# Moving modulation-weight chunks from TensorE to VectorE in a two-layer diffusion trunk step (60 to 116 of 192)

## The chip, the cores and the metric

The kernel runs on one core of a Trainium2 chip. The metric is device time in microseconds for one execution of the whole program; lower is better.

## The reference: what is computed

Two layers over 128 context and 128 latent tokens, width 2048, all in fp32. Each layer has six modulation vectors of 2048 features for each of two conditioning vectors, then attention and a squared-ReLU MLP, each between modulated norms:

```python
def modulation(cvec, w_ada_l, b_ada_l):
    m = jax.nn.silu(cvec) @ w_ada_l + b_ada_l
    return jnp.split(m[:, None, :], N_MOD, axis=-1)
...
sh_a, sc_a, gt_a, sh_m, sc_m, gt_m = modulation(c, w_ada[l], b_ada[l])
h = rms_norm(xs, g_pre_a) * (1.0 + sc_a) + sh_a
...
xs = xs + gt_a * rms_norm(o, g_post_a)
h = rms_norm(xs, g_pre_m) * (1.0 + sc_m) + sh_m
xs = xs + gt_m * rms_norm(squared_relu_mlp(h, w_up[l], w_down[l]), g_post_m)
```

`w_ada` of one layer is 2048 x 12288, so the modulation is a product of two rows with 201 MB of weights over both layers: 192 chunks of 128 x 2048 fp32 (1 MB). The attention mixes three head groups (neighbourhood, grouped-query, differential) and one output projection.

## The kernel before

**Chunks.** Everything that is streamed comes in 1 MB chunks: 360 "trunk" chunks (projection in, projection out, MLP up and down) and 192 modulation chunks. SyncE's queue (SP) loads them in one fixed order into five buffers `raw` (`issue`, L994 to L1001); a load is issued when the chunk in its buffer is released. For a trunk chunk, `split_to` (L1003) makes of each half a high part `wh` on ScalarE (L1011) and the residue `wl` on VectorE (L1012), three buffers each, and TensorE multiplies three times (L361 to L363 with tokens stationary, L395 to L397 with weights stationary).

**Modulation on TensorE** (`ada_mm`, L126): 132 chunks. Four fp32 matmuls of 128 x 32 by 128 x 512 fill the four column strips of the array (L131). In the trace each of them is two rows, so a chunk is x8 there; in the order of a program it is x4. After four chunks ScalarE copies the bank to `pt` (L135), and TensorE transposes it (scale and shift) or, for a gate block, sums it with a selector (L153). 12 of the 132 chunks are held in idle `XT` buffers (`ahead`, L749).

**Modulation on VectorE** (`dv_mul`, L196): 60 chunks, in the two MLPs only. The weights lie transposed, features on partitions; `sB` holds silu(c) of both vectors on every partition. One chunk is four products of 1024 columns with a running sum (L204): two vectors by two halves. The last one writes back into `raw` and releases it.

**Order.** A list `items` fixes the order of the program, and each engine works through its own instructions in that order, apart from shifts that the scheduler of the framework makes when it builds the program. `weave` (L765) spreads modulation chunks evenly among the trunk chunks of a stretch. Attention, and `dv_mul`, are generators that are advanced by some steps after each half trunk chunk (L1054 to L1056):

```python
step_list(fast, 1)
step_list(slow, 2)
step_list(dvq, 1 + (len(dvq) > 1))
```

`slow` is attention and `dvq` the VectorE chunks. Before `w_out` may read a head group, `need` (L857) runs that group's generator to its end.

**Stages.** Layer 0 builds its normalized input a quarter at a time (`make_xt`), with the modulation blocks just ahead of it; all four input groups therefore finish late, and its attention runs from about 244 us to 413 us, beside the last input groups and the first part of `w_out`. Layer 1 has its modulation ready and runs group after group. x is stored to DRAM at the start of each MLP (`store_x`) and read back near its end (`load_x`), since `sB` takes two of the four `stg` buffers there.

Of the kernel before, what the change touches and what calls it, by code (L numbers as in the profile page):

```python
# [12 lines left out]
BF16 = mybir.dt.bfloat16  # L13
# [6 lines left out]
L = 2  # L20
# [17 lines left out]
C_ID, C_SEL, C_GC, C_GS, C_DC, C_DS, C_MK, C_LO, C_SV, C_END = 0, 128, 160, 288, 416, 480, 544, 608, 609, 865  # L38


def _consts():
    c = np.zeros((P, C_END), np.float32)
    c[:, C_ID:C_ID + P] = np.eye(P, dtype=np.float32)
    for g in range(4):
        for v in range(2):
            c[32 * g + v, C_SEL + v] = c[32 * g + v, C_SEL + 2 + v] = 1.0
# [22 lines left out]
def trunk(ctx: ExitStack, tc: tile.TileContext, I, O):  # L69
# [31 lines left out]
    def rstd(out, ss, n, width):  # L101
        """out = (ss / n + eps) ** -0.5"""
# [20 lines left out]
    # ---------------------------------------------------------------- ada  # L123
# [14 lines left out]
    gcs = {}  # L138

    def ada_post(l, sec, blk, pt):  # L140
        if sec in (2, 5):
            w = 0 if sec == 2 else 1
            if blk == 0:
                gb = sb([P, 512], "gb")
                gg = sb([P, 512], "gg")
                nc.sync.dma_start(gb, I["gb"][l, w])
                nc.sync.dma_start(gg, I["gg"][l, w])
                gcs[(l, w)] = (sb([P, 512], "gc", dt=F32R), gb, gg)
            gc, gb, gg = gcs[(l, w)]
            yield  # L150
            m = psm()
            r = slice(32 * blk, 32 * blk + 32)
            pe.matmul(m[r, :], cs[:, C_SEL:C_SEL + 32], pt, start=True, stop=True, tile_position=(0, 32 * blk))  # L153
            yield
            t, h = sb([P, 512], "tmp", NTMP), sb([P, 512], "tmp", NTMP, F32R)
            dve.tensor_tensor(t[r, :], m[r, :], gb[r, :], ALU.add)
            dve.tensor_tensor(t[r, :], t[r, :], gg[r, :], ALU.mult)
            act.activation(h[r, :], t[r, :], AF.Copy)
            dve.scalar_tensor_tensor(gc[r, :], h[r, :].bitcast(F32), cs[r, C_LO:C_LO + 1], t[r, :], ALU.mult, ALU.add)
        else:  # L160
            yield
            m = psm()
            for j in range(4):
                tr(m[:, j * P:(j + 1) * P], pt[:, j * P:(j + 1) * P])
            yield
            red = st1[:, 0:8].rearrange("p (j v) -> p j v", v=2)
            dve.tensor_reduce(red, m.rearrange("p (j g c) -> p j c g", g=4, c=32)[:, :, 0:2, :], AX.X, ALU.add)
# [17 lines left out]
    # the same product on the vector engine: features on partitions, c along the free axis  # L185
    sB = [None, None]
    dv_live = {}

    def load_sb():
        for v in range(2):  # L190
            sB[v] = sb([P, D], "stg", 4)
# [941 lines left out]
```

## Time and profile before

| what | us |
|---|---|
| median of 3 runs | 2409.05 (2407.94 to 2409.51) |
| profiled execution, its span | 2406.6 |
| TensorE busy (matmuls) | 2337.6 |
| VectorE busy | 1489.0 |
| ScalarE busy | 1109.7 |

The span runs from the first to the last instruction of one profiled execution. It is 2.45 us below the median; the three runs carry no trace, and a row of the trace is always one of the profiled execution. Busy time is the time in which an engine had at least one instruction under way. In rows of matmuls in time, the second number is a modelled duration; what a matmul adds to its neighbours is read from the distance of starts. In the MLPs DMA moved 203 to 279 GB/s, in layer 0's attention stage about 300.

### The profile page before, as it was taken

How to read it: one execution, taken by the hardware profiler on the slowest of the kernel's cores; microseconds unless marked ns; L12 is line 12 of the kernel's file. 1: busy time of each engine (PE TensorE's matmuls, PEld its weight loads, DVE VectorE, ACT ScalarE, POOL GpSimd, SP SyncE). 2: the span in 40 equal slices, each digit the busy share in tenths (PEclk: the TensorE clock that was granted, in tenths of full speed). 3: DMA queues.
4: the chain of work that ended last, by engine and by line, in shares of the span. 5: the costliest groups of instructions: out<-in, count | busy, mean ns of one | idle time of the engine just before them, and what ended most of it. 6: DMA issues, size and time to landing. Idle time of an engine off the chain costs nothing.

```text
span 2406.6 us, 33407 instructions
## 1 busy us (share of the span) xinstructions
PE 2337.6 (97%) x13584; PEld 1898.3 (79%) x13584; DVE 1489.0 (62%) x2078; ACT 1109.7 (46%) x1533; POOL 22.8 (1%) x30
## 2 busy tenths in 40 slices
PE   6999999989999999999999999999999999999998
PEld 3666666679789789889867777777988988988986
DVE  2455765367867878878455565546665566565545
ACT  3433454365444444435445454547544543543543
POOL 0000000000000000000000000000000000000000
PEclk8999999999999999999999999999999999999999
DMA  9778788876877877777676765776566566556652
GB/s 362 277 308 303 286 313 306 324 269 244 316 265 291 291 276 282 283 293 275 225 283 217 248 219 210 288 262 245 208 214 226 195 219 226 200 211 228 235 184 88
DMA packets 93650, 613.45 MB, mean 255 GB/s; under 512 B 13880, under 2 KB 16312, under 8 KB 20280
## 3 DMA queue, kind: packets, MB, share of 16 engines
q1 hardware_dynamic: 92776, 610.70, 69.5%
q8 instruction: 106, 1.74, 0.3%
q10 hardware_dynamic: 720, 0.62, 0.1%
q14 instruction: 48, 0.39, 0.0%
HBM read 599.49 MB, written 11.79 MB: 254 GB/s over the span
## 4 chain that ended last, share of the span: by engine, by line
PE 93%; DVE 2%; ACT 2%; DMA 1%; issue 1%; POOL 0%; ACTq 0%; POOLq 0%; DVEq 0%
PE acc L361 18%; PE acc L362 18%; PE acc L363 18%; PE acc L395 10%; PE acc L397 10%; PE acc L396 10%; PE ada L131 4%; PE m L107 2%; DVE wl L1012 1%; PE m L483 1%; DMA ngT<-ngT_in 1%; PE m L153 0%; PE m L517 0%; ACT stg L331 0%; PE m L302 0%
## 5 line engine op out<-in xcount | busy, mean ns | idle before, releaser
L1012 DVE TENSOR_TENSOR wl<-raw,wh 128x1024 fp32r<-128x1024 f32 x720 | 876.2, 1223 | 590.8 <-ACT wh L1011 586.9
L1011 ACT ACTIVATE wh<-raw 128x1024 fp32r<-128x1024 f32 x720 | 760.3, 1059 | 978.1 <-PE acc L363 615.2
L395 PE MATMUL acc<-XT,wh 128*128 128x256 f32 x2048 | 580.8, 284 | 2.8 <-ACT XT L277 2.8
L397 PE MATMUL acc<-XT,wl 128*128 128x256 f32 x2048 | 579.0, 283 | 0.5 <-DVE wl L1012 0.5
L396 PE MATMUL acc<-XT,wh 128*128 128x256 f32 x2048 | 577.8, 282 | 0.3 <-DVE XT L278 0.3
L361 PE MATMUL acc<-wh,big 128*128 128x512 f32 x1280 | 508.4, 400 | 0.0
L362 PE MATMUL acc<-wl,big 128*128 128x512 f32 x1280 | 506.0, 395 | 0.5 <-DVE wl L1012 0.5
L363 PE MATMUL acc<-wh,big 128*128 128x512 f32 x1280 | 505.0, 395 | 0.0
L395 PEld LDWEIGHTS acc<-XT,wh 128*128 128x128 f32 x2048 | 387.0, 189 | 14.0 <-issue 8.6
L396 PEld LDWEIGHTS acc<-XT,wh 128*128 128x128 f32 x2048 | 387.5, 189 | 0.7 <-DVE XT L278 0.5
L397 PEld LDWEIGHTS acc<-XT,wl 128*128 128x128 f32 x2048 | 386.7, 189 | 0.7 <-DVE wl L1012 0.7
L361 PEld LDWEIGHTS acc<-wh,big 128*128 128x128 f32 x1280 | 240.4, 188 | 80.9 <-issue 24.8
L363 PEld LDWEIGHTS acc<-wh,big 128*128 128x128 f32 x1280 | 240.9, 188 | 56.6 <-issue 0.7
L362 PEld LDWEIGHTS acc<-wl,big 128*128 128x128 f32 x1280 | 241.1, 188 | 55.8 <-DVE wl L1012 2.5
L361 PE MATMUL acc<-wh,XT 128*128 128x512 f32 x576 | 236.9, 414 | 9.5 <-ACT XT L277 7.0
L362 PE MATMUL acc<-wl,XT 128*128 128x512 f32 x576 | 230.0, 399 | 0.8 <-DVE wl L1012 0.7
L363 PE MATMUL acc<-wh,XT 128*128 128x512 f32 x576 | 228.3, 398 | 0.0
L361 PEld LDWEIGHTS acc<-wh,XT 128*128 128x128 f32 x576 | 109.0, 190 | 72.6 <-issue 25.6
L131 PE MATMUL ada<-raw,sT 128*32 128x512 f32 x960 | 136.6, 618 | 13.6 <-ACT sT L120 7.8
L204 DVE SCALAR_TENSOR_TENSOR tmp<-raw,stg 128x1024 bf16<-128x1024 f32 x120 | 144.8, 1218 | 2.5 <-DMA raw<-w_adaT_in 2.3
L204 DVE SCALAR_TENSOR_TENSOR raw<-raw,stg 128x1024 f32<-128x1024 f32 x120 | 145.4, 1219 | 0.1
L362 PEld LDWEIGHTS acc<-wl,XT 128*128 128x128 f32 x576 | 109.7, 190 | 27.3 <-DVE wl L1012 3.5
(140 smaller groups left out, 1243.7 us busy)
## 6 DMA issues: line engine op xcount, KB each, us to landing
raw<-w_up_in SPq DMA_DIRECT2D x128, 1024.0 KB, 4.8
raw<-w_down_in SPq DMA_DIRECT2D x128, 1024.0 KB, 4.8
raw<-w_ada_in SPq DMA_DIRECT2D x120, 1024.0 KB, 6.5
raw<-w_in_in SPq DMA_DIRECT2D x72, 1024.0 KB, 4.8
raw<-w_adaT_in SPq DMA_DIRECT2D x60, 1024.0 KB, 4.9
raw<-w_out_in SPq DMA_DIRECT2D x32, 1024.0 KB, 4.8
XT<-w_ada_in SPq DMA_DIRECT2D x12, 1024.0 KB, 8.8
xd<-stg SPq DMA_DIRECT2D x6, 1024.0 KB, 9.0
```

Of the source, the lines that this page charges most:

```text
L107: pe.transpose(out, in_, ident)
L131: pe.matmul(pa[32 * g:32 * g + 32, :], sT[:, 4 * kq + g, :], raw[:, g * 512:(g + 1) * 512], start=(kq == 0), stop=(kq == 3), tile_position ...
L204: dve.scalar_tensor_tensor(o, raw[:, c], 1.0, sB[v][:, c], ALU.mult, ALU.mult, accum_out=a[:, j, v, h:h + 1])
L361: pe.matmul(a, xh, wh[:, c], start=first, stop=False)
L362: pe.matmul(a, xh, wl[:, c], start=False, stop=False)
L363: pe.matmul(a, xl, wh[:, c], start=False, stop=last)
L395: pe.matmul(a, wh[:, c], xh, start=first, stop=False)
L396: pe.matmul(a, wh[:, c], xl, start=False, stop=False)
L397: pe.matmul(a, wl[:, c], xh, start=False, stop=last)
L483: pe.matmul(m[:, i * keys:(i + 1) * keys], qT[:, h, :], kT(h), start=True, stop=True)
L1011: act.activation(wh, r, AF.Copy)
L1012: dve.tensor_tensor(wl, r, wh.bitcast(F32), ALU.subtract)
```

## The change

Of the 192 chunks 116 instead of 60 go to VectorE, and 76 instead of 132 stay on TensorE:

| stretch | TensorE before | after | VectorE before | after |
|---|---|---|---|---|
| layer 0, attention stage | 80 | 56 | 0 | 24 |
| layer 0, MLP (and its end) | 20 | 4 | 44 | 64 |
| layer 1, attention stage | 32 | 16 | 0 | 12 |
| layer 1, MLP | 0 | 0 | 16 | 16 |

A VectorE chunk is two products of 2048 columns instead of four of 1024 (the first writes to a one-byte buffer `junk`), its steps are given out by a credit of a half or one per half trunk chunk, and at most two such chunks wait: a third forces steps at once. TensorE's chunks are placed two by two. `sB` is a constant loaded once, during the first projection, so that x stays in `stg` through the MLPs: four stores and four loads of 1 MB, and three loads each of `gb` and `gg`, are gone. In the MLPs VectorE's chunks begin after the third trunk chunk instead of after the tenth and later.

```diff
+G_A, G_M = [(2, b) for b in range(4)], [(5, b) for b in range(4)]
+M_A = [(i, f) for f in range(4) for i in range(2)]
+M_M = [(3 + i, f) for f in range(4) for i in range(2)]
+DV_BLOCKS = [G_A + M_M[:2] + G_M, M_A + M_M[:4] + G_A[:3] + G_M]
+PE_BLOCKS = [M_A + M_M[2:], M_M[4:] + G_A[3:]]
...
+    sB = [const.tile([P, D], F32, name=f"sB{v}") for v in range(2)]
...
         for v in range(2):
-            for h in range(2):
-                c = slice(h * 1024, (h + 1) * 1024)
-                o = raw[:, c] if v else sb([P, 1024], "tmp", NTMP, BF16)
-                dve.scalar_tensor_tensor(o, raw[:, c], 1.0, sB[v][:, c], ALU.mult, ALU.mult,
-                                         accum_out=a[:, j, v, h:h + 1])
-                if v and h:
-                    release()
-                yield
+            o = raw if v else sb([P, D], "junk", 1, FP8)
+            dve.scalar_tensor_tensor(o, raw, 1.0, sB[v], ALU.mult, ALU.mult, accum_out=a[:, j, v:v + 1],
+                                     saturate=None if v else False)
+            if v:
+                release()
+            yield
...
-                while used < nf and used * nt < t * nf:
-                    items.append(fill[used])
-                    used += 1
+                while used < nf and (used + 1) * nt < t * nf:
+                    items.extend(fill[used:used + 2])
+                    used += 2
+                while done < len(dv) and done * nt < t * len(dv):
+                    items.append(dv[done])
+                    done += 1
...
-                    weave(ch, ada_items(l, [(0, f + 1), (1, f + 1)]))
+                    weave(ch, ada_items(0, M_A[2 * f + 2:2 * f + 4]), dv[:3] if f else ())
+                    dv = dv[3:] if f else dv
                 else:
-                    weave(ch, fill[:N3])
-            weave(c2, fill[N3:N2])
+                    weave(ch, fill[:4], dv[:6])
+            weave(c2, fill[4:6], dv[6:10])
...
-        weave(rest, fill, TAIL)
+        cut = 8 if l == 0 else 40
+        nf = (len(fill) - TAIL) * cut // len(rest) // 2 * 2
+        weave(rest[:cut], fill[:nf], dv)
+        weave(rest[cut:], fill[nf:], tail=TAIL)
...
-                if (q, nt, s) == (3, 1, 1):
-                    load_x()
...
-                if q == g == 0:
-                    rest.insert(3, ("call", store_x))
...
+            g, m = dv_items(0, G_M), dv_items(1, M_A + M_M[:4])
+            dv = [x for i in range(16) for x in m[3 * i:3 * i + 3] + g[i:i + 1]]
+            weave(rest[:2], [])
+            weave(rest[2:118], [], dv)
...
+            while len(dvq) > 2:
+                step_list(dvq, 1)
...
-                step_list(dvq, 1 + (len(dvq) > 1))
+                state["credit"] += 0.5 + 0.5 * (len(dvq) > 1)
+                if state["credit"] >= 1.0:
+                    step_list(dvq, 1)
+                    state["credit"] -= 1.0
```

**VectorE, differential attention of the latent tokens in layer 0** (the end of the attention stretch; `st` are softmax sums, `big` probabilities or a head group's output, line numbers of each kernel). Before:

```order
L638 TENSOR_SCALAR st_2633<-st_2633,lam 128x2
L628 TENSOR_REDUCE st_2653<-m 128x2
L641 TENSOR_SCALAR big<-big,st_2633 128x256 x2
L642 SCALAR_TENSOR_TENSOR big<-big,st_2633 128x256 x2
L637 RECIPROCAL st_2654<-st_2654 128x2 x2
L638 TENSOR_SCALAR st_2654<-st_2654,lam 128x2
L641 TENSOR_SCALAR big<-big,st_2654 128x256 x2
L642 SCALAR_TENSOR_TENSOR big<-big,st_2654 128x256 x2
L657 COPY big<-m 128x512
L669 TENSOR_REDUCE st_2689<-tmp 128x4
```

and after:

```order
L627 SCALAR_TENSOR_TENSOR big<-big,st_2689 128x256 x2
L189 SCALAR_TENSOR_TENSOR junk,aacc<-raw,sB_89 128x2048
L642 COPY big<-m 128x512
L189 SCALAR_TENSOR_TENSOR raw,aacc<-raw,sB_90 128x2048
L204 MEMSET gt 128x128
L654 TENSOR_REDUCE st_2724<-tmp 128x4
L189 SCALAR_TENSOR_TENSOR junk,aacc<-raw,sB_89 128x2048
L107 TENSOR_SCALAR st_2724<-st_2724 128x4
L189 SCALAR_TENSOR_TENSOR raw,aacc<-raw,sB_90 128x2048
L660 SCALAR_TENSOR_TENSOR tmp<-m,st_2724,bcs 128x128 x4
L451 TENSOR_TENSOR big<-m,big 128x4x128
```

The same steps of attention now have a 2048-wide product (L189) between nearly each two of them.

**TensorE at the same place**, right after the context products of that head group (L664 or L649); the transposes that follow are L107 or L111. Before:

```order
L664 MATMUL m<-cv,big 128x128
L131 MATMUL ada<-raw,sT 32x512 x7
L107 MATMUL m<-cs,tmp 128x128
L107 MATMUL m<-cs,stg 128x128 x2
L107 MATMUL m<-cs,tmp 128x128
```

and after:

```order
L649 MATMUL m<-cv,big 128x128
L135 MATMUL ada<-raw,sT 32x512 x3
L111 MATMUL m<-cs,tmp 128x128 x2
L111 MATMUL m<-cs,stg 128x128
L111 MATMUL m<-cs,tmp 128x128 x2
```

Seven modulation matmuls stood between the products and the transposes that wait for VectorE; three are left.

**VectorE, layer 0's first steps of the MLP** (`XT` is the MLP's input, built by `make_xt`). In the changed kernel:

```order
L254 TENSOR_SCALAR big<-m,mod_2_77,mod_3_78 128x128 x4
L262 TENSOR_TENSOR XT_3504<-big,XT_3504 128x2x128 x3
L242 TENSOR_SCALAR big<-stg,st_3522 128x512
L262 TENSOR_TENSOR XT_3504<-big,XT_3504 128x2x128
L189 SCALAR_TENSOR_TENSOR junk,aacc<-raw,sB_89 128x2048
L254 TENSOR_SCALAR big<-m,mod_2_77,mod_3_78 128x128 x4
L262 TENSOR_TENSOR XT_3505<-big,XT_3505 128x4x128
```

A product now stands among the steps that build the MLP's input; before, the first product came after ten trunk chunks.

## Rows read from the trace of the kernel before

**Rows 1.** First lines of the page, and its chain of waits.

```profile
span 2406.6 us, 33407 instructions
...
PE 2337.6 (97%) x13584; PEld 1898.3 (79%) x13584; DVE 1489.0 (62%) x2078; ACT 1109.7 (46%) x1533; POOL 22.8 (1%) x30
...
PE 93%; DVE 2%; ACT 2%; DMA 1%; issue 1%; POOL 0%; ACTq 0%; POOLq 0%; DVEq 0%
```

**Rows 2.** Windows by stage: us, busy us (instructions) per engine, granted clock, DMA share, GB/s.

```profile
0.00:244.00 244.00, 215.08 (x1028) 141.06 (x1029) 115.31 (x175) 95.61 (x138) 1.44 (x6) 0.97 0.82 312
244.00:317.00 73.00, 72.59 (x356) 45.83 (x354) 50.61 (x91) 32.21 (x58) 4.29 (x3) 1.00 0.80 293
317.00:413.00 96.00, 92.59 (x508) 59.20 (x505) 51.47 (x112) 44.04 (x106) 2.01 (x2) 1.00 0.80 303
413.00:486.00 73.00, 66.74 (x334) 42.96 (x332) 32.16 (x55) 29.99 (x54) 1.67 (x3) 0.99 0.87 337
515.00:1255.00 740.00, 739.48 (x4673) 646.12 (x4676) 552.97 (x729) 339.53 (x385) 0.00 (x0) 1.00 0.76 279
1290.00:1643.00 353.00, 351.78 (x1662) 255.98 (x1664) 188.11 (x277) 165.77 (x274) 6.87 (x6) 1.00 0.67 241
1660.00:2407.00 747.00, 735.10 (x4657) 661.06 (x4655) 438.93 (x503) 345.63 (x399) 1.10 (x2) 0.99 0.57 203
```

**Rows 3.** Instruction groups by line: count | busy us, mean ns | idle before.

```profile
L1012 DVE TENSOR_TENSOR wl<-raw,wh 128x1024 fp32r<-128x1024 f32 x720 | 876.2, 1223 | 590.8 <-ACT wh L1011 586.9 <-PE m L234 1.6
...
L131 PE MATMUL ada<-raw,sT 128*32 128x512 f32 x960 | 136.6, 618 | 13.6 <-ACT sT L120 7.8 <-DMA raw<-w_ada_in 5.1 <-ACT pt L135 0.7
...
L914 DVE TENSOR_TENSOR big<-tmp,big 128x512 fp32r<-128x512 f32 x64 | 44.1, 689 | 81.4 <-ACT big L913 81.4
...
L153 PE MATMUL m<-pt,cs 128*32 128x512 f32 x24 | 12.5, 605 | 0.0
```

**Rows 4.** TensorE in time: start us, us; one chunk alone, first layer's MLP.

```profile
618.11 0.40 PE L363 MATMUL acc<-wh,big 128*128 128x512 f32 x1
618.43 1.07 PE L131 MATMUL ada<-raw,sT 128*32 128x512 f32 x8
619.43 0.51 PE L361 MATMUL acc<-wh,big 128*128 128x512 f32 x1
619.77 0.39 PE L362 MATMUL acc<-wl,big 128*128 128x512 f32 x1
```

**Rows 5.** TensorE in time: two chunks in one run, first layer's w_out.

```profile
326.91 0.39 PE L363 MATMUL acc<-wh,big 128*128 128x512 f32 x1
327.23 1.92 PE L131 MATMUL ada<-raw,sT 128*32 128x512 f32 x16
329.08 0.51 PE L361 MATMUL acc<-wh,big 128*128 128x512 f32 x1
329.43 0.39 PE L362 MATMUL acc<-wl,big 128*128 128x512 f32 x1
```

**Rows 6.** VectorE in time, first layer's MLP: products, a residue, a 512-wide step.

```profile
610.77 1.22 DVE L204 SCALAR_TENSOR_TENSOR tmp<-raw,stg 128x1024 bf16<-128x1024 f32 x1
...
611.91 1.22 DVE L1012 TENSOR_TENSOR wl<-raw,wh 128x1024 fp32r<-128x1024 f32 x1
...
899.78 0.69 DVE L914 TENSOR_TENSOR big<-tmp,big 128x512 fp32r<-128x512 f32 x1 [2.61 <-ACT big L913]
900.38 1.22 DVE L204 SCALAR_TENSOR_TENSOR tmp<-raw,stg 128x1024 bf16<-128x1024 f32 x1
```

**Rows 7.** Windows of 10 us at the start: columns as in rows 2.

```profile
20.00:30.00 10.00, 4.38 (x32) 1.08 (x28) 0.63 (x5) 3.12 (x9) 0.00 (x0) 0.96 1.01 421
```

**Rows 8.** VectorE's waits, 520 to 1270 us: us in total, times, longest.

```profile
DVE wl L1012 <- ACT wh L1011: 131.5, 94, 6.1
DVE big L914 <- ACT big L913: 39.1, 15, 3.8
```

**Rows 9.** The DMA queue's own waits, 60 to 490 us.

```profile
SPq L998 <- PE ada L131: 204.7, 60, 9.5
```

More of the change, by code (lines that the diff above doesn't have):

```diff
@@ L138, in trunk @@
     gcs = {}
+    made = set()
     def ada_post(l, sec, blk, pt):
-        if sec in (2, 5):
[L142 to L149, printed above, removed]
-            yield
[L151 to L159, printed above, removed]
-        else:
[L161 to L167, printed above, removed]
+        yield
+        m = psm()
+        for j in range(4):
+            tr(m[:, j * P:(j + 1) * P], pt[:, j * P:(j + 1) * P])
+        yield
+        red = st1[:, 0:8].rearrange("p (j v) -> p j v", v=2)
+        dve.tensor_reduce(red, m.rearrange("p (j g c) -> p j c g", g=4, c=32)[:, :, 0:2, :], AX.X, ALU.add)
+        if sec in (2, 5):
+            yield from gate_fin(l, sec, blk, red)
+        else:
             mod_fin(l, sec, blk, red)
@@ L226, in gate_fin @@
         dve.tensor_copy(gt[:, :, 2:4], gt[:, :, 0:2])
-        if blk == 0:
-            gcs[(l, w)] = (sb([P, 512], "gc", dt=F32R),)
-        gc = gcs[(l, w)][0]
+        if (l, w) not in gcs:
+            gcs[(l, w)] = sb([P, 512], "gc", dt=F32R)
+        gc = gcs[(l, w)]
         yield
@@ L239, in gate_fin @@
         dve.scalar_tensor_tensor(gc[r, :], h[r, :].bitcast(F32), cs[r, C_LO:C_LO + 1], m[r, :], ALU.mult, ALU.add)
+        made.add((l, w, blk))
     XT = [None] * 4
@@ L733, in call, with ada_items, dv_items @@
         items.append(("call", fn))
-    def ada_items(l, secblks):
-        return [("ada", I["w_ada"][l, sec * 4 + blk, kq], (l, sec, blk, kq)) for sec, blk in secblks for kq in range(4)]
-    def dv_items(l, w):
-        blocks = modblocks(0) + modblocks(1) + gateblocks(1)
-        return [("dv", I["w_adaT"][blocks.index(b), j], (l, *b, j)) for b in w for j in range(4)]
-    def modblocks(w):
-        return [(3 * w + i, f) for f in range(4) for i in range(2)]
-    def gateblocks(w):
-        return [(3 * w + 2, b) for b in range(4)]
+    def ada_items(l, blocks):
+        return [("ada", I["w_ada"][_pe_no(l, b), kq], (l, *b, kq)) for b in blocks for kq in range(4)]
+    def dv_items(l, blocks):
+        return [("dv", I["w_adaT"][_dv_no(l, b), j], (l, *b, j)) for b in blocks for j in range(4)]
     def ahead(ada):
@@ L938, in trunk @@
         if l + 1 < L:
-            load, use = ahead(ada_items(1, modblocks(1)[NDV:NDV + 1]))
+            load, use = ahead(ada_items(1, M_M[4:5]))
         rest = []
@@ L986, in trunk @@
     raws = {}
-    state = {"dma": 0, "live": 0, "split": 0}
+    state = {"dma": 0, "live": 0, "split": 0, "credit": 0.0}
     subs = [(i, j) for i, it in enumerate(chunks) if it[0] == "t" for j in range(2)]
@@ L1074, in _layout @@
     g["ngT"] = _f(ng.reshape(L, 4, KT, P).transpose(3, 0, 1, 2))
-    gb = np.zeros((L, 2, 4, 32, 512), np.float32)
-    gg = np.zeros((L, 2, 4, 32, 512), np.float32)
-    for w in range(2):
-        for r in range(4):
-            gb[:, w, :, r] = ba.reshape(L, 6, 4, 512)[:, 2 + 3 * w]
-            gg[:, w, :, r] = ng.reshape(L, 4, 4, 512)[:, 1 + 2 * w]
-    g["gb"], g["gg"] = gb.reshape(L, 2, P, 512), gg.reshape(L, 2, P, 512)
     g["qg"], g["kg"], g["dg"] = _f(v["gqa_q_g"]), _f(v["gqa_k_g"]), _f(v["diff_g"])
@@ L1092, in tiles @@
         return w.reshape(l, k // (P * kt), kt, P, n).transpose(0, 1, 3, 2, 4).reshape(l, k // (P * kt), P, kt * n)
-    wa = v["w_ada"].reshape(L, 4, 4, P, 24, 512).transpose(0, 4, 1, 3, 2, 5)
-    g["w_ada"] = _f(wa.reshape(L, 24, 4, P, 2048))
-    wt = v["w_ada"][1].reshape(D, 2, 3, 4, 4, P).transpose(1, 3, 2, 4, 5, 0)
-    g["w_adaT"] = _f(np.concatenate([wt[:, :, :2].reshape(16, 4, P, D), wt[1, :, 2].reshape(4, 4, P, D)]))
+    wa = v["w_ada"].reshape(L, 4, 4, P, 6, 4, 512).transpose(0, 4, 5, 1, 3, 2, 6)
+    g["w_ada"] = _f(np.stack([wa[l][b].reshape(4, P, 2048) for l in range(L) for b in PE_BLOCKS[l]]))
+    wt = v["w_ada"].reshape(L, D, 6, 4, 4, P).transpose(0, 2, 3, 4, 5, 1)
+    g["w_adaT"] = _f(np.stack([wt[l][b] for l in range(L) for b in DV_BLOCKS[l]]))
     g["crow"] = _f(np.stack([v["c_ctx"].reshape(D), v["c"].reshape(D)]))
```

76 lines of the change are left out of this document (34 added, 42 removed).

## The prediction

> **What bounds the kernel now.** I read the page first, then windows by stage, then TensorE and VectorE in time, then the waits. TensorE is busy for 97% of the span and makes up 93% of the chain of waits [rows 1]. By stage it is full nearly everywhere: 739.5 of 740 us in layer 0's MLP, 351.8 of 353 in layer 1's attention stage, 72.6 of 73 and 92.6 of 96 in layer 0's attention [rows 2]. So a matmul taken out of TensorE's order gives its time back, as long as TensorE doesn't then wait for what VectorE or DMA deliver. VectorE is busy for 62% [rows 1], but 553 of 740 us in layer 0's MLP [rows 2]. The first 244 us are the one stretch where TensorE is visibly short of work (215 us busy), at 312 GB/s and a DMA share of 0.82 [rows 2].
>
> **What a chunk costs on TensorE.** Projection matmuls start 0.23 us apart. Around a lone chunk the last matmul before it starts at 618.11 and the second one after it at 619.77; without it that would be 0.46 us, so the chunk adds 1.20 us [rows 4]. Two in one run add 329.43 - 326.91 - 0.46 = 2.06 us [rows 5]. A run of n chunks therefore costs 0.34 + 0.86 n. (The group's busy time, 136.6 us for 120 chunks, is 1.14 each [rows 3].) By the order of TensorE's instructions the 132 chunks come in 109 runs, the 76 in 41:
> - before: 109 x 0.34 + 132 x 0.86 = 150.6 us; after: 41 x 0.34 + 76 x 0.86 = 79.3 us; 71.3 us less.
> - Layer 0's attention stage: 63 runs of 80 chunks become 34 of 56: -30.5 us.
> - Layer 0's MLP: 16 lone chunks go: -19.2 us. Layer 1's attention stage, with the chunks at its start: 30 runs of 36 become 7 of 20: -21.6 us.
>
> Follow-up work on TensorE: every gate block has one short group of matmuls of about 1 us (12.5 us for the 12 on TensorE's side [rows 3]), and the changed order has as many, 16, on whichever engine the products run: nothing. Scale and shift blocks that are transposed fall from 21 to 19, four 128-wide transposes each, about 1 us in all, which I leave out.
>
> **What it costs on VectorE.** Successive 1024-wide steps start 1.14 us apart (610.77, 611.91), a 512-wide one 0.60 us ahead of its successor (899.78, 900.38) [rows 6]: 0.54 us for each further 512 columns, so a 2048-wide product takes 1.14 + 2 x 0.54 = 2.22 us. No row has such a width or a one-byte output: at least 2.16 (no fixed part), at most 2.44 (two of the busy 1.22). A product that writes bf16 and a residue that writes fp32 both show 1.22 [rows 6], so the output's size should not matter, and I take 2.22. A chunk is 4.44 us on VectorE (before 4 x 1.14 = 4.56); 116 chunks are 515 us in place of 274. The question is where these 241 us have room.
>
> **Layer 0's MLP.** VectorE's 553 us [rows 2] lose 44 x 4.56 = 201 and gain 64 x 4.44 = 284, with some 4 us of gate steps: 640 us, in a stage that should take 740 - 19 = 721, so 89%. Its waits there for ScalarE (131.5 us for `wh`, 39.1 for the MLP's activation [rows 8]) are mostly those of an engine that is ahead, and shrink when it is late. In order, a product of 2.22 us can now stand in front of a residue that TensorE needs, and only two halves (2.8 us each) are prepared ahead. Cost between 0 and 20 us (the saving gone); I take 6, nearer to 0 since 11% stays free.
>
> **Layer 1's attention stage.** VectorE 188 of 353 us [rows 2] plus 12 x 4.44 = 53: 241 of about 331. Room enough; 4 us for products in front of attention steps (0 to 10).
>
> **Layer 0's attention, 244 to 413 us.** By VectorE's order 30 products lie between the first head norm and the last head group's output. VectorE was busy 50.6 + 51.5 = 102.1 us in these 169 us [rows 2]; with 30 x 2.22 = 66.6 it is 168.7. That is the whole stretch. TensorE's own work there falls by about 18.5 us (26.25 chunks become 9.25, and some 12 runs fewer: 17 x 0.86 + 12 x 0.34), and the chunks that go are those that filled the gaps while a softmax step went from engine to engine. So VectorE and the chain of attention set the length: about 160 at best (each step's busy time holds some 0.08 us that overlap its successor), and 169 + 33 = 202 if half of VectorE's old idle time (67 us) remains idle. I take 175, nearer to the lower end since products are many small pieces that fit into most waits. That is +6 instead of -18.5. `need` makes it sharper: `w_out` waits behind the last steps of each head group, and TensorE behind it.
>
> **The first 244 us.** TensorE's saving there is 7.5 of the 30.5 us. DMA has to bring more to the same point: 29.3 trunk chunks, 34 + 9 modulation chunks and 2 MB for `sB`, against 28.5 + 36, about 10 MB beyond 312 GB/s x 244 us = 76.1 MB. 86.6 MB in 236.5 us is 366 GB/s; three 10 us windows at the start moved some 420 (421 in [rows 7]), at which it would take 206 us. I take the 7.5 as gained. The Trainium skill (DMA: Bandwidth & Descriptors, Specifications) gives about 358 GB/s as one core's limit to HBM, which speaks against this change: by it the stretch would take 242 us, and the gain below would be 5.5 us smaller. The trace does not agree with the page (421 [rows 7]), and I go by the row. 413 to 486 us: TensorE's saving of about 5 us holds, DMA having less to bring.
>
> **Small terms.** A product now stands among the steps that build each MLP's input, where TensorE waits for VectorE: +2 us each (0 to 4.4), 4 together. Eight 1 MB transfers of x less: they lie beside full TensorE at 203 to 279 GB/s [rows 2], nothing.
>
> **Sum**, against the profiled 2406.6 us: attention of layer 0 -30.5 + 18.5 + 6 = -6.0; MLP of layer 0 -19.2 + 6 = -13.2; layer 1's attention -21.6 + 4 = -17.6; inputs of the MLPs +4: -32.8 us. From the median of 2409.05 (2.45 above the profiled span) that is 2376.
>
> **Rivals.**
> - *VectorE is never in the way* (20%): all of the 71.3 us and more pairing, 2337. For: 11 to 27% of VectorE's time stays free outside layer 0's attention. Against: the 168.7 of 169 us there.
> - *Five buffers, not DMA, hold the first stretch* (8%, slower): a VectorE chunk keeps its buffer until its second product, which comes by credit, so loads are issued late; SP already waited 204.7 us for buffers of TensorE's chunks there [rows 9]. If the old 312 GB/s is the most that five buffers carry, 86.6 MB take 278 us, 41 more than taken: -32.8 + 41 = +9, 2418. It decides below about 321 GB/s. Against: the 421 of [rows 7], with the same five buffers.
> - *Attention at its upper end* (8%): the stretch takes 202, not 175, +27: 2403, and with the MLP's stall at 20 us 2417.
> - *DMA itself holds the first stretch* (4%): at the 337 GB/s of the busiest later stage [rows 2] its 86.6 MB take 257 us, 20 more than taken: 2397. Against: a share of 0.87 in that row, which leaves more. The limit on the page of the Trainium skill named above would make it 242 us, and the time 2382.
> - *It does not do what it says* (2%): the lone chunks come back as waits for VectorE one by one, 2409. The order shows the 76 chunks and 232 products as told.
>
> **How the numbers follow.** My forecast has 58%. Its own range, from the ends of the stall terms, is 2355 to 2400. The range asked for reaches to the first rival's neighbourhood and to the lower half of the third: 2340 to 2406. A measurement of this kernel tells about 0.2% (4.8 us). Faster by more: 58 + 20 + 4 and 2 of the third, 84%. Within: 4 of the third and the last 2, 6%. Slower: 8 + 2, 10%.
>
> **What would show it.** In the changed profile: 2048-wide products of 2.2 to 2.3 us; layer 0's MLP near 728 us with TensorE idle for a few us, released by `wl`; layer 1's attention stage near 335; layer 0's attention stretch near 175 with VectorE almost full and TensorE waiting for steps of softmax; the first stretch near 237 at over 350 GB/s. Wrong would be: products above 2.5 us (VectorE then sets the MLP's pace), a first stretch beyond 260 us with DMA's share still at 0.8, or an attention stretch that shrinks with TensorE's share.

## The result, and the profile after

The changed kernel takes 2424.84 us (median of 4 runs, 2420.71 to 2432.12); the kernel before, beside it, 2409.06. The ratio is 1.0072 with a 95% interval of 1.0053 to 1.009: 15.8 us slower, where 2376 was forecast. The profiled execution is the shortest of the four, 2420.71 us with a span of 2418.6.

First lines of the page of the changed kernel, which answer to [rows 1]:

```profile
span 2418.6 us, 32541 instructions
...
PE 2301.6 (95%) x13200; PEld 1915.8 (79%) x13200; DVE 1704.7 (70%) x2093; ACT 1096.0 (45%) x1514; POOL 33.2 (1%) x30
...
PE 87%; DVE 6%; DMA 2%; issue 2%; ACT 2%; POOL 1%; ACTq 0%; POOLq 0%; DVEq 0%
```

TensorE is busy 36.0 us less, though its modulation matmuls alone take 65.1 us less (151.2 before, 86.1 after): its other matmuls take longer. And yet the span is 12.0 us longer: TensorE's share of the chain fell from 93 to 87%, and VectorE's rose from 2 to 6%. The windows by stage, with the columns of [rows 2], say where:

```profile
0.00:244.00 244.00, 194.26 (x904) 129.58 (x904) 133.66 (x196) 91.70 (x130) 1.44 (x6) 0.92 0.83 321
244.00:317.00 73.00, 70.43 (x312) 50.84 (x312) 62.68 (x96) 28.69 (x48) 4.63 (x2) 0.97 0.72 260
317.00:413.00 96.00, 82.46 (x354) 56.61 (x356) 86.05 (x152) 36.49 (x85) 5.50 (x2) 0.82 0.73 276
413.00:486.00 73.00, 60.40 (x275) 42.19 (x267) 45.11 (x68) 28.07 (x54) 2.96 (x1) 0.91 0.64 238
545.00:1262.00 717.00, 715.37 (x4575) 644.59 (x4574) 623.90 (x645) 334.00 (x385) 0.00 (x0) 1.00 0.76 282
1300.00:1645.00 345.00, 342.01 (x1616) 267.57 (x1615) 234.57 (x347) 173.20 (x286) 9.16 (x5) 1.00 0.64 234
1660.00:2418.00 758.00, 742.71 (x4704) 665.94 (x4696) 446.45 (x464) 348.86 (x417) 2.02 (x4) 0.99 0.55 199
```

The clock column tells as much as the busy ones: of these stages only those before 545 us have a granted clock below 0.98. In 317 to 413 us VectorE is busy 86.1 of 96 us (before 51.5), TensorE 82.5 instead of 92.6, at a mean granted clock of 0.82.

Fixed windows blur what moved, so I take three events as marks and read their starts from the rows of their lines: the last piece of the input's last quarter (ScalarE's `XT`), the last head group's output (VectorE's `big`), the first matmul of layer 0's MLP. A row is the line, its count, durations, first and last start, forms. Of the kernel before:

```profile
L277 ACT ACTIVATE XT<-big x10: 401/621/637, 33.5 to 217.7; 128x512 fp32r<-128x512 f32 x6, 128x256 fp32r<-128x256 f32 x4
...
L466 DVE TENSOR_TENSOR big<-m,big x8: 691/691/693, 284.2 to 408.7; 128x512 fp32r<-128x512 f32 x8
...
L395 PE MATMUL acc<-XT,wh x256: 274/281/416, 497.8 to 595.7; 128*128 128x256 f32 x128
```

Of the changed one:

```profile
L261 ACT ACTIVATE XT<-big x10: 402/621/631, 33.4 to 243.4; 128x512 fp32r<-128x512 f32 x6, 128x256 fp32r<-128x256 f32 x4
...
L451 DVE TENSOR_TENSOR big<-m,big x8: 686/692/697, 309.9 to 462.5; 128x512 fp32r<-128x512 f32 x8
...
L380 PE MATMUL acc<-XT,wh x205: 274/281/415, 541.0 to 619.8; 128*128 128x256 f32 x103
```

With the same kind of marks behind layer 0's MLP (first input matmul of layer 1: 1268.4 before, 1298.9 after) and layer 1's attention (first matmul of its MLP: 1657.0 and 1669.5) the whole difference is laid out. The forecast's terms are sorted by the same marks:

| stretch | before | after | change | forecast |
|---|---|---|---|---|
| start to last `XT` | 217.7 | 243.4 | +25.7 | -7.5 |
| to the last head group's output | 191.0 | 219.1 | +28.1 | +6 |
| to the MLP's first matmul | 89.1 | 78.5 | -10.6 | -2.5 |
| layer 0's MLP, and its end | 770.6 | 757.9 | -12.7 | -13.2 |
| layer 1's attention stage | 388.6 | 370.6 | -18.0 | -15.6 |
| layer 1's MLP, to the end | 749.6 | 749.1 | -0.5 | 0 |
| sum | 2406.6 | 2418.6 | +12.0 | -32.8 |

From layer 0's MLP on all came as forecast. Layer 0's attention stage (the first three rows) is 43.2 us longer instead of 4.0 shorter, and that is the whole miss (47.2 us, of which the later stages take back 2.4).

What VectorE does there, in time (start us, us; a part of the last quarter's `make_xt` in the changed kernel):

```profile
235.99 0.18 DVE L152 TENSOR_REDUCE st<-m 128x8 f32<-128x32 f32 x1
236.11 2.29 DVE L189 SCALAR_TENSOR_TENSOR raw<-raw,sB 128x2048 f32<-128x2048 f32 x1
...
238.33 0.23 DVE L168 SCALAR_TENSOR_TENSOR mod<-st,baT 128x4 f32<-128x4 f32 x2
238.48 1.22 DVE L989 TENSOR_TENSOR wl<-raw,wh 128x1024 fp32r<-128x1024 f32 x1
239.61 0.23 DVE L169 TENSOR_TENSOR mod<-mod,ngT 128x4 f32<-128x4 f32 x2
239.76 2.29 DVE L189 SCALAR_TENSOR_TENSOR junk<-raw,sB 128x2048 fp8e5<-128x2048 f32 x1
...
241.97 1.36 DVE L254 TENSOR_SCALAR big<-m,mod,mod 128x128 f32<-128x128 f32 x4
243.25 0.68 DVE L262 TENSOR_TENSOR XT<-big,XT 128x512 fp32r<-128x512 f32 x1
243.85 2.28 DVE L189 SCALAR_TENSOR_TENSOR raw<-raw,sB 128x2048 f32<-128x2048 f32 x1
...
246.06 0.69 DVE L262 TENSOR_TENSOR XT<-big,XT 128x512 fp32r<-128x512 f32 x1
```

From the sum of a modulation block (L152) to the `XT` that TensorE waits for, three products stand between steps of 0.2 to 1.4 us. And what a wait costs on TensorE, a quarter earlier (in brackets: idle us before it, and what ended that):

```profile
174.85 0.79 PE L346 MATMUL acc<-wh,XT 128*128 128x512 f32 x1 [4.24 <-ACT XT L261]
175.44 0.63 PE L347 MATMUL acc<-wl,XT 128*128 128x512 f32 x1
175.87 0.63 PE L348 MATMUL acc<-wh,XT 128*128 128x512 f32 x1
...
180.13 0.40 PE L346 MATMUL acc<-wh,XT 128*128 128x512 f32 x1
180.37 0.39 PE L347 MATMUL acc<-wl,XT 128*128 128x512 f32 x1
```

After 4.24 us of idling successive matmuls start 0.43 us apart, until 180.13; then 0.23 us. These are its two clocks, 1.2 and 2.4 GHz: the twelve matmuls after this wait took 5.3 instead of 12 x 0.23 = 2.8 us. The granted clock was 1.00 in 160 to 172 us, which hold two shorter waits (0.72 and 1.94 us), and 0.50 in 174 to 180. The Trainium skill (TensorE: Matmul & The Clock Gate, What's actually happening) has the array's clock halved after idling and restored by activity; these rows agree.

### The profile page after: what moved, and what is told of

Same layout as the page of the kernel before. It is cut to its first block, busy times and chain, and to the rows that moved or that the text cites. A ratio compares the mean times of both kernels' runs of the same rounds, so it can differ in the third digit from the quotient of the medians.

```text
span 2418.6 us, 32541 instructions
## 1 busy us (share of the span) xinstructions
PE 2301.6 (95%) x13200; PEld 1915.8 (79%) x13200; DVE 1704.7 (70%) x2093; ACT 1096.0 (45%) x1514; POOL 33.2 (1%) x30
## 4 chain that ended last, share of the span: by engine, by line
PE 87%; DVE 6%; DMA 2%; issue 2%; ACT 2%; POOL 1%; ACTq 0%; POOLq 0%; DVEq 0%
PE acc L346 17%; PE acc L347 17%; PE acc L348 17%; PE acc L382 9%; PE acc L381 9%; PE acc L380 9%; PE ada L135 2%; PE m L111 2%; DVE wl L989 2%; DVE junk L189 1%; POOL st L108 1%; DVE raw L189 1%; PE m L217 1%; DMA ngT<-ngT_in 1%; PE m L468 1%
## 5 line engine op out<-in xcount | busy, mean ns | idle before, releaser
L189 DVE SCALAR_TENSOR_TENSOR junk<-raw,sB 128x2048 fp8e5<-128x2048 f32 x116 | 265.1, 2285 | 32.2 <-DMA raw<-w_adaT_in 32.1
L189 DVE SCALAR_TENSOR_TENSOR raw<-raw,sB 128x2048 f32<-128x2048 f32 x116 | 264.9, 2284 | 0.1
L346 PE MATMUL acc<-wh,XT 128*128 128x512 f32 x576 | 236.0, 417 | 25.5 <-ACT XT L261 18.6
L347 PE MATMUL acc<-wl,XT 128*128 128x512 f32 x576 | 235.5, 410 | 9.5 <-DVE wl L989 9.3
L346 PEld LDWEIGHTS acc<-wh,XT 128*128 128x128 f32 x576 | 111.7, 195 | 67.1 <-ACT XT L261 20.7
L348 PEld LDWEIGHTS acc<-wh,XT 128*128 128x128 f32 x576 | 111.9, 195 | 26.5 <-DVE XT L262 1.5
```

Source lines behind the costliest of these rows:

```text
L189: dve.scalar_tensor_tensor(o, raw, 1.0, sB[v], ALU.mult, ALU.mult, accum_out=a[:, j, v:v + 1], saturate=None if v else False)
L346: pe.matmul(a, xh, wh[:, c], start=first, stop=False)
L347: pe.matmul(a, xh, wl[:, c], start=False, stop=False)
L348: pe.matmul(a, xl, wh[:, c], start=False, stop=last)
```

## The experiments

Theories of the 43.2 us: **VectorE's work** (its products delay steps that TensorE waits for; by their sum, by their place, or by the length of one piece), **buffers** (a VectorE chunk holds one of five load buffers, so loads come late), **cover** (the matmuls that left had filled TensorE's waits). Each run names the difference to its own runs of the kernel before (median 2407.4 to 2408.5); for the change itself that is +15.8 us. The marks of all runs:

| run | last `XT` | last output | MLP | to the kernel before |
|---|---|---|---|---|
| kernel before | 217.7 | 408.7 | 497.8 | |
| change | 243.4 | 462.5 | 541.0 | +15.8 |
| e1, all 24 back | 220.0 | 407.1 | 503.1 | -23.1 |
| e2, early 12 back | 220.2 | 434.7 | 520.3 | -6.6 |
| e3, late 12 back | 242.1 | 425.2 | 509.7 | -17.0 |
| e4, 128 wide | 222.3 | 410.3 | 488.6 | -39.4 |
| e5, chain cleared | 236.3 | 463.4 | 541.2 | +13.6 |
| e6, cover | 241.5 | 458.1 | 538.0 | +9.0 |
| e7, 128 wide, longer hold | 220.8 | 408.9 | 487.3 | -40.4 |
| e8, 1024 wide | 230.0 | 416.7 | 493.4 | -36.5 |
| e9, two pieces | 236.6 | 452.4 | 529.7 | +3.8 |
| e13, one vector | 227.1 | 413.7 | 490.6 | -27.6 |

**e1: the 24 chunks of layer 0's attention stage back on TensorE.**

```diff
-DV_BLOCKS = [G_A + M_M[:2] + G_M, ...
-PE_BLOCKS = [M_A + M_M[2:], ...
+DV_BLOCKS = [G_M, ...
+PE_BLOCKS = [M_A + G_A + M_M, ...
-            fill = ada_items(0, M_M[2:])
-            dv = dv_items(0, G_A + M_M[:2])
+            fill = ada_items(0, G_A + M_M)
+            dv = []
```

> Undoes one part: the 24 VectorE chunks of layer 0's attention stage go back to TensorE, two by two; the MLPs, layer 1 and sB loaded in the first projection stay as in the change. In the changed kernel the first matmul of layer 0's MLP starts at 541.0 us (before 497.8). Every theory that puts the loss on these 24 chunks (VectorE's order, held buffers, lost cover) expects that start near 490 to 498 and 2420.7 - 43 to 51 = 2370 to 2378 in all. If the loss came from something else of the change in this stage (sB's load, x kept in SBUF, pairs of TensorE's chunks), the start stays at 520 or later and the time above 2400.

2384.22 us, ratio 0.9902 (0.9887 to 0.9916). The MLP starts at 503.1: the loss goes with the 24 chunks, but for 5 us that stay against the kernel before (last `XT` +2.3, from there to the last output -3.9, the end of the stage +6.9). The time is some 6 us over what was expected by that. It beats both kernels.

**e2 and e3: only the early, only the late half back.** The same edit with `G_A[:3]`, or with `G_A[3:] + M_M[:2]`.

> Undoes half of it: only the first 12 of the 24 (those woven into the first 244 us, up to the last quarter of the input) go back to TensorE, the later 12 stay on VectorE. In the changed kernel the last quarter's XT came 25.7 us late and the rest of the stage lost 17.5 us more. If each half pays for itself, the time is about 2395 (2420.7 - 26). If the stage is one budget of VectorE (order theory with VectorE full at 244 to 413), the early 12 going away frees little there, and it is 2390 to 2400; if it is buffers alone, early chunks cost most and it is 2380 to 2390.

> The other half: the later 12 of the 24 (beside the last small projection and the first half of w_out, where attention runs) go back to TensorE, the first 12 stay on VectorE. If each half pays for itself: last XT still at about 243, the stretch from there to the last head group's output 195 instead of 219, 2400 to 2405 in all. If the early half sets the length alone (attention merely starts later), the time is nearly that of the changed kernel, 2415.

2400.80 us (ratio 0.995 to 0.9978) and 2390.37 us (0.9912 to 0.9941). The early half back undoes the late `XT` (220.2); but the stretch to the last output is still 214.5 us long. The late half back leaves the late `XT` (242.1) and the stretch behind it is 183.1. So the two halves cost in two places. Either one alone wins more than its share (22 and 33 us against the change, both together 39), so some 16 us are lost only where both are there. Neither expectation came true: e2 is just above the slowest of its cases, and e3 is 10 us faster than either of its two.

**e4: products 128 columns wide.**

```diff
+        n = slice(0, 128 if l == 0 and sec < 5 else D)
-            dve.scalar_tensor_tensor(o, raw, 1.0, sB[v], ...
+            dve.scalar_tensor_tensor(o[:, n], raw[:, n], 1.0, sB[v][:, n], ...
```

> Leaves out 15/16 of the sums of these 24 chunks: their products are 128 instead of 2048 columns wide; loads, steps, places and releases stay. VectorE's work in the stage falls by 48 x 2.1 = 101 us; TensorE's stays at the changed kernel's, without the 24 chunks. Order theory (the 2.28 us of each product in the order of VectorE): MLP of layer 0 starts at 470 to 495, the time is 2350 to 2375. Buffer theory (chunks hold one of five buffers from load to product) and cover theory (TensorE has nothing to do in its waits any more): the start stays at 525 or later, the time above 2400. Between them, the share of the 43 us that goes is the share of the order theory.

2367.91 us; the MLP starts at 488.6, 52.4 us earlier than in the changed kernel. All of the loss goes with VectorE's time, and with what a shorter product brings along: its chunk's buffer comes free earlier (see e7). It also shows what TensorE's 24 chunks were worth there: without them, and with products that take almost no time, the stage is only 9.2 us shorter than before, and 14.5 shorter than in e1, which has the rest of the change.

The whole stage from 60 us to the MLP's first matmul (columns as in [rows 2]); kernel before, changed kernel, e4:

```profile
60.00:497.80 437.80, 416.28 (x2085) 271.93 (x2083) 240.90 (x416) 187.72 (x326) 9.39 (x9) 0.99 0.81 302
60.00:541.00 481.00, 417.75 (x1909) 287.10 (x1907) 339.43 (x531) 188.10 (x322) 16.20 (x9) 0.91 0.74 280
60.00:488.60 428.60, 396.53 (x1906) 277.74 (x1904) 248.89 (x527) 185.78 (x319) 9.47 (x9) 0.96 0.80 310
```

In the changed kernel TensorE is busy as long as before, 417.8 and 416.3 us, though 24 chunks have left it: what they saved went into matmuls at the lower clock (mean granted clock 0.91 instead of 0.99). The stage's 43.2 us are nearly all idle time of TensorE, 63.3 us instead of 21.5. So the loss is in both, in TensorE's waits and in a clock that is down after some of them, as after the 4.24 us shown above. How much the clock would cost by itself was not tried.

**e5: no product in the norm's chain.**

```diff
-                while done < len(dv) and done * nt < t * len(dv):
+                while done < len(dv) and (done < t - late if late else done * nt < t * len(dv)):
...
-                    weave(ch, ada_items(0, M_A[2 * f + 2:2 * f + 4]), dv[:3] if f else ())
+                    weave(ch, ada_items(0, M_A[2 * f + 2:2 * f + 4]), dv[:3] if f else (), late=1)
...
-                    weave(ch, fill[:4], dv[:6])
+                    weave(ch, fill[:4], dv[:6], late=2)
```

> The changed kernel with the same 24 VectorE chunks, but inside layer 0's first projection each quarter's chunks are woven in from its second (last quarter: third) trunk chunk on instead of evenly, so that no product stands any more among VectorE's steps from a modulation sum to the XT that TensorE waits for (six stood there or right ahead). VectorE's work, loads and number of buffers are the same. If the place of the products in that chain is what made the last XT 25.7 us late (order theory, as latency): XT's last at 222 to 232, the time 2405 to 2412. If what counts there is VectorE's whole load, or buffers held, or lost cover: last XT stays at 238 or later and the time within 5 us of 2421.

2422.05 us, ratio 1.0056 (1.0041 to 1.0071): nothing gained. The rows of the chain above had made me think of this first, and it fell. The last `XT` does come 7.1 us earlier (236.3, between the two cases expected), and the last output comes at 463.4 all the same: some products are only done later (12 start before that mark instead of 15), in a stretch where VectorE has no room.

**e6: idle matmuls on TensorE.**

```diff
+            if it[2][0] == 0 and it[2][1] < 5:
+                cover()
```

(`cover` is four matmuls of 128 x 32 by 128 x 512 with zero weights.)

> The changed kernel with idle work added on TensorE: at the place of each of the 24 VectorE chunks of layer 0's attention stage it runs four matmuls of a chunk's shape (zero weights, constants as data, no load), 20.6 us by the 0.86 us of a further chunk, up to 28.8 us alone. Cover theory (TensorE waits anyway there, and falls to 1.2 GHz after each wait): they cost 0 to 5 us, or give some back, with a higher granted clock in 120 to 480 us. If TensorE's own work still set the pace between the waits: 2438 to 2450.

2417.51 us, ratio 1.0038 (1.0025 to 1.0051): 33.6 us of added matmuls cost nothing; the profiled execution is 3.0 us shorter than the change's (span 2415.6), and by the differences to the kernel before e6 is 6.8 us faster. The added work, as a group of instructions (count | busy us, mean ns):

```profile
L136 PE MATMUL ada<-cs,zw 128*32 128x512 f32 x192 | 33.6, 626 | 1.0 <-ACT pt L148 0.7
```

Windows of the changed kernel and of e6 (columns as in [rows 2]):

```profile
300.00:360.00 60.00, 52.87 (x240) 39.37 (x239) 55.90 (x94) 25.12 (x54) 2.44 (x1) 0.91 0.82 309
360.00:420.00 60.00, 50.14 (x208) 31.86 (x206) 54.02 (x94) 21.50 (x56) 3.06 (x1) 0.79 0.67 246
```

```profile
300.00:360.00 60.00, 58.74 (x291) 40.81 (x289) 57.17 (x98) 25.31 (x57) 2.45 (x1) 1.00 0.86 322
360.00:420.00 60.00, 50.39 (x232) 27.54 (x232) 53.22 (x90) 20.43 (x52) 1.85 (x1) 0.83 0.64 240
```

TensorE is busy 5.9 us more in the first of them, at a granted clock of 1.00 instead of 0.91. So in the changed kernel the matmuls of 24 chunks are free on TensorE, and a higher clock goes with them; but cover gives back only 3 of the stage's 43 us.

**e7: a longer hold.** As e4, with two more idle steps between a chunk's two products.

```diff
+            if not v and l == 0 and sec < 5:
+                yield
+                yield
```

> As the run with 128-wide products (it leaves out 15/16 of the sums of these 24 chunks; 2367.9 us), but with two more idle steps between a chunk's two products, so that each of these chunks keeps its load buffer about twice as long. Buffer theory: a longer hold of one of five buffers makes loads late and costs 10 us or more (2378 and up). If buffers are not what decides: within 4 us of 2368.

2368.10 us, 0.2 us from e4. But the hold did not get longer. In both traces the same steps of VectorE stand between a chunk's two products, which start 0.3 us apart in most chunks (2.3 us or more in the changed kernel), and from the issue of its load to its release a chunk takes 14.2 us on average in both (25.5 in the changed kernel). So e7 says nothing on buffers, and e4 has a shorter hold as well as a shorter product.

What speaks on buffers is the waiting for late loads. ScalarE's waits for loaded trunk chunks, from 60 us to the MLP's start (us in total, times, longest); changed kernel, then e5:

```profile
ACT wh L988 <- DMA raw<-w_in_in: 31.4, 9, 5.1
ACT wh L988 <- DMA raw<-w_out_in: 6.6, 2, 3.3
```

```profile
ACT wh L988 <- DMA raw<-w_in_in: 17.5, 9, 4.7
ACT wh L988 <- DMA raw<-w_out_in: 3.7, 2, 2.4
```

Together 38.0 us in the changed kernel and 7.4 in the kernel before, so loads do come later. But the stage's length does not follow them: e5 has 21.2 us and a stage as long as the change's, e4 28.5 us and a stage that is 52.4 us shorter, and e9 (below) holds its chunks longest, 28.6 us on average, in a stage that is 11.3 us shorter. With TensorE's own 2.8 us in the changed kernel (none in e4) these waits differ by 12.3 us between the two, so as an estimate late loads hold at most a small part of the 52.4 us. That buffers have no part at all isn't shown.

**e8, e9, e13: how VectorE's time counts.** e8 is e4 with 1024 columns. e9 cuts each product into two of 1024 with sums of their own; e13 runs one product for each chunk instead of two:

```diff
-        for v in range(2):
+        for v in range(1 if l == 0 and sec < 5 else 0, 2):
```

> As the run with 128-wide products, but 1024 wide (leaves out half of the sums of these 24 chunks). A product is then 1.14 instead of 2.28 us. With 128 columns the MLP of layer 0 starts at 488.6 us, with 2048 at 541.0. If each product simply costs a share of its length wherever it stands: start near 514, time near 2394. If it is VectorE running full (92% busy at 300 to 360 us, 90% at 360 to 420) that decides, half the length takes it out of that and the start is below 503, the time below 2383.

> The changed kernel with each of the 48 products of layer 0's attention stage cut into two of 1024 columns with sums of their own (added at the end). VectorE's work there is the same plus some 6 us (48 x 0.06, and four small additions); only the longest piece between two other steps is halved. If VectorE's whole load sets the stage: no gain, MLP of layer 0 starts at 538 to 548, the time 2420 to 2430. If the length of one uninterrupted piece decides (a step that TensorE needs waits behind 2.28 us): the start comes 15 us or more earlier, the time below 2408.

> The changed kernel with one product of 2048 columns for each of the 24 chunks of layer 0's attention stage instead of two (it leaves out one of the two conditioning vectors in these chunks). VectorE's work there is halved as with 1024-wide products (2372.0 us, MLP of layer 0 from 493.4), but each piece still takes 2.28 us. If the sum of VectorE's work decides: start at 491 to 498, the time 2368 to 2378. If the length of a piece decides, each of the 24 that are left costs what each of the 48 did (1.1 us of the stage): start near 515, the time near 2395.

2371.98, 2411.83 and 2379.80 us. Half the work at half the length starts the MLP at 493.4, half the work at full length at 490.6: the sum decides. Both also shorten a chunk's hold, to 18.2 and 15.3 us. (e13's time is 8 us more than that of e8; its MLP of layer 0 takes 10 us longer, which I did not follow up.)

Cutting pieces at equal work (e9) wins 11.3 of the 43 us, between its two expected cases: the length of a piece is a second, smaller cause.

The window between the first two marks shows how the length follows VectorE's work. Kernel before, e8, e13, changed kernel, e9:

```profile
217.70:408.70 191.00, 186.47 (x955) 121.14 (x958) 115.76 (x219) 84.38 (x172) 6.31 (x5) 1.00 0.80 299
```

```profile
230.00:416.70 186.70, 173.96 (x828) 124.86 (x832) 149.05 (x303) 80.81 (x166) 8.11 (x5) 0.95 0.78 297
```

```profile
227.10:413.70 186.60, 175.24 (x828) 127.44 (x832) 148.18 (x270) 79.79 (x166) 9.12 (x5) 0.93 0.78 297
```

```profile
243.40:462.50 219.10, 189.79 (x835) 132.15 (x838) 180.99 (x301) 80.27 (x165) 13.10 (x5) 0.88 0.68 254
```

```profile
236.60:452.40 215.80, 183.13 (x828) 133.06 (x832) 188.43 (x380) 80.30 (x166) 10.61 (x5) 0.88 0.70 259
```

With 115.8, 149.1 or 148.2 us of VectorE's work the stretch takes 187 to 191 us; with 181.0 it takes 219.1, which is the work and 38 us; e5, with 187.8, takes 227.1, the work and 39. So up to about 150 us products are free here, and at 181 and above the stretch is as long as the work and some 38 idle us of VectorE that are not used; with halved pieces 27. Between the two this does not hold: e2, with 163.6 us of work, takes 214.5, the work and 51. What sets its length stays open.

**e10 to e12, e14, e15: versions.** e10 is e1 with three edits. It moves `sB`'s load beside the second half of `w_out` and spreads TensorE's last chunks; the third is left out here:

```diff
-TAIL = 4
+TAIL = 0
-                    ch.insert(4, ("call", load_sb))
+                    rest.append(("call", load_sb))
```

> A version meant to beat both: the run with all 24 chunks back on TensorE (2384.2 us), with sB loaded beside the second half of w_out instead of the first projection, TensorE's last chunks of an attention stage spread evenly instead of four kept for after w_out, and the transposes of the block that is held in the XT buffers put behind the first quarter of the MLP's input. In that run TensorE stood idle 5.4 us before the held block and started the MLP 13 us after the last norm factor was ready. If these waits are the price of the tail: 2370 to 2378. If TensorE only waits for the norm instead: within 4 us of 2384.

2384.88 us: no gain over e1. The last `XT` comes at 218.2, so `sB` did cost 2 us, but with 2 MB more beside `w_out` its loads come later (ScalarE waits for them 17.5 us in 400 to 510, 11.2 in e1).

e11 adds two blocks of layer 1 to VectorE:

```diff
-            dv = dv_items(1, G_A[:3])
+            dv = dv_items(1, G_A + M_M[5:6])
```

> As the version before it, and in layer 1's attention stage 20 instead of 12 chunks on VectorE (8 more, 35.5 us of products; VectorE then 270 of 345 us, TensorE 8 fewer chunks). There all input groups follow one another and TensorE is busy 342 of 345 us, so theory says that removed matmuls count: -7 us against the version before it. If VectorE's steps get late as in layer 0: +0 to +10.

2380.34 us: 8 more chunks of layer 1 on VectorE win 4.5 of the 7 us.

e12 is e10 with layer 0's chunks one by one:

```diff
+                while one and used < nf and used * nt < t * nf:
+                    items.append(fill[used])
+                    used += 1
```

> As the first of the two versions, with layer 0's attention-stage chunks on TensorE placed one by one as in the kernel before instead of two by two. By the start-up cost of a run, 0.34 us, some 25 more runs are 8.5 us: slower by 5 to 9 if TensorE's own work counts there. If in this stage TensorE mostly waits and single chunks cover more waits: within 3 us, or faster.

2385.62 us, within 1 us of e10; its MLP starts 6.4 us earlier (495.5), and takes that much longer. Whether single chunks are worth more than pairs stays open.

e14 is e1 with the edits of e11 and e12, and `sB` loaded in two parts:

```diff
+                    rest.insert(5, ("call", lambda: load_sb([1])))
+                    rest.insert(2, ("call", lambda: load_sb([0])))
```

> A version meant to beat both: all 24 chunks of layer 0's attention stage on TensorE, one by one; 20 instead of 12 chunks of layer 1's attention stage on VectorE; sB loaded in two parts beside the first half of w_out; the ends of the attention stages as in the changed kernel. MLP of layer 0 from about 496 (495.5 with single chunks), from there to layer 1's MLP 1129 - 5 (the 8 further chunks gave -4.5 us), and 749 to the end: 2370 + 2.5 = 2370 to 2375. If single chunks merely move their waits into the MLP, as in the run before it (2385.6 against 2384.9): 2378 to 2382.

2370.81 us (2369.43 to 2371.77), ratio 0.9847 (0.9834 to 0.9861): the fastest version, 36.6 us below the kernel before. Its page:

```profile
span 2368.7 us, 32793 instructions
...
PE 2292.1 (97%) x13344; PEld 1901.1 (80%) x13344; DVE 1638.3 (69%) x2033; ACT 1101.9 (47%) x1522; POOL 26.5 (1%) x30
```

It keeps the change in layer 0's MLP and enlarges it in layer 1, and leaves layer 0's attention stage to TensorE; VectorE is busy for nearly as much of the span as in the changed kernel (69 and 70%), but at other places.

e15 adds one block of layer 0 to VectorE:

```diff
+        dv = dv_items(0, M_M[4:5]) if l == 0 else []
```

> As the version before it, with 4 more chunks of layer 0 on VectorE, beside the second half of w_out, where attention is over and VectorE is busy 20 of 60 us and TensorE 58. Theory (room on VectorE, TensorE full): -3 to -5 us, 4 lone chunks at 1.2. If their products get in the way of the norm at the stage's end: +2 to +6.

2372.60 us: 4 further chunks beside the second half of `w_out` bring nothing. The MLP starts 3.0 us earlier and the time is 1.8 us higher, within the spread of its runs (2370.26 to 2375.13).

## Why the prediction was wrong

**Cost of a product: right.** 2.22 us was taken; the rows say 2285 ns, with starts 2.21 us apart, and the one-byte output makes no difference:

```profile
L189 DVE SCALAR_TENSOR_TENSOR junk<-raw,sB 128x2048 fp8e5<-128x2048 f32 x116 | 265.1, 2285 | 32.2 <-DMA raw<-w_adaT_in 32.1
L189 DVE SCALAR_TENSOR_TENSOR raw<-raw,sB 128x2048 f32<-128x2048 f32 x116 | 264.9, 2284 | 0.1
```

**Layer 0's MLP: right.** 623.9 of 717 us of VectorE (forecast 640 of 721), TensorE idle for 1.6 us, and its change -12.7 instead of -13.2. VectorE's waits in 545 to 1262 us, against [rows 8], are those of an engine that is ahead less often:

```profile
DVE wl L989 <- ACT wh L988: 60.6, 69, 2.0
DVE junk L189 <- DMA raw<-w_adaT_in: 22.1, 19, 2.6
...
DVE big L898 <- ACT big L897: 1.6, 1, 1.6
```

**Layer 1's attention stage: right**, -18.0 for -15.6.

**The first 244 us: the step that failed first.** It priced DMA against TensorE, and took TensorE's 7.5 us as gained. The products that run in this stretch had no term at all (48 less the 30 counted in attention leaves 18; in the trace 15 start before the last `XT`, 34.4 us of VectorE), though VectorE is the engine that turns each modulation sum into the input TensorE waits for, and adds up each quarter's outputs. They cost 21.1 us (last `XT` at 243.4, with 128-wide products 222.3; 7.7 us at half the length, 4.8 with half as many); with the norm's chain cleared of them (e5) 7.1 of it goes, and how the rest divides stays open. Even the 7.5 was not there: with e4's products the mark is 4.6 us later than before. Of DMA the step was right that 312 GB/s was no limit: the changed kernel moved 321 GB/s in the first row above, e4 with the same loads 340 up to its last `XT`. The 366 GB/s that it needed were not tried there; e10 shows more in a later stretch, over 60 us:

```profile
420.00:480.00 60.00, 55.88 (x298) 32.91 (x297) 16.76 (x29) 14.20 (x16) 0.00 (x0) 1.00 0.97 388
```

388 GB/s at a share of 0.97, beside the 421 of [rows 7]. The Trainium skill (DMA: Bandwidth & Descriptors, Specifications) gives about 358 GB/s for one core; its section Bandwidth keeps that figure for two cores that stream from one HBM domain at once, and has 425 GB/s measured for one alone. This kernel runs on one core, and the measured 388 and 421 are above the first figure and below the second.

**Layer 0's attention: the right mechanism, the wrong end.** The step counted 168.7 us of VectorE's work for a stretch of 169, gave 160 and 202 as bounds, and took 175, "since products are many small pieces that fit into most waits". They do not: of VectorE's old idle time between the first two marks (75 us) half stays idle (38 us), which is what the upper end assumed. By marks, +28.1 for +6, with 33 products in the stretch. What was said to be sharp, that VectorE would be nearly full with TensorE waiting, was to be seen (VectorE at 55.9 and 54.0 of 60 us in the windows above).

**TensorE's saving in this stage** was the third miss: -30.5 us before the stalls, of which the sum kept 12.0. e4 shows 9.2 us as its worth without VectorE's part (14.5 against e1), and e6 shows that in the changed kernel as much work can be put back for nothing. That the chunks that left had stood in waits, which they covered at a granted clock of 1.00 [rows 2], is argued from this. It holds up to the last output, where e4 is 1.6 us later than the kernel before. Behind it the saving is there, and larger than priced: -10.6 for -2.5 us (e4 -10.8), with about 5 chunks fewer. Why a chunk is worth some 2 us there isn't shown.

**Range and rivals.** The upper ends of the four stall terms lie 27, 14, 6 and 4.8 us above what was taken; together they give 2428, so 2355 to 2400 was too narrow for the forecast's own terms. That 2428 is near the measured time is luck, since the first stretch has no part in it. The outcome is the attention's upper end together with a loss in the first stretch. The rival for that stretch came near in time (2418; by its own terms 2417, since -32.8 + 41 is 8) by another mechanism, five buffers: loads did come later, but the stage's length does not follow them (see e7). That VectorE is never in the way was excluded by e4, a limit of DMA at 337 GB/s by the rows above. No case held that both stretches fail at once, and for the one engine common to both that should have been a case.

## What to carry to other kernels

Work for an engine with idle time is free only up to a point that is below its idle time: here about 150 of 190 us in a stretch of dependent steps, while 87% busy did no harm in a stream of independent chunks; so price each stretch by its kind, and price every stretch in which an instruction is added. An engine that is 97% busy in a stretch of waits may be filled with cover: what leaves it there is worth little, while in a stretch that it really bounds it is worth most of its price (12.7 of 19.2 us in layer 0's MLP, 18.0 of 21.6 in layer 1's attention stage). Give the other engine work where the stream is independent, and leave the dependent stretch alone (e14: 36.6 us faster, where the full change lost 15.8).

## What was unexpected of the hardware

With 24 chunks gone from layer 0's attention stage TensorE was busy there for as long as before (417.8 and 416.3 us), at a mean granted clock of 0.91 instead of 0.99. Adding 33.6 us of idle matmuls made the kernel 3 to 7 us faster, at a higher granted clock (1.00 instead of 0.91 in 300 to 360 us); that the clock is the reason fits the rows, and was not tried by itself. One wait of 4.24 us cost 2.5 us more in the matmuls behind it.
